# One transformer-like kernel: longer runs of context products in the MoE, and attention scores with both passes on all 128 rows

## The chip, the cores and the metric

The kernel runs on one core of a Trainium2 chip. Its time is the device time of one execution in microseconds (us), and the figure compared is the median of the runs. The engines are TensorE (PE in the rows, with PEld for its weight loads), VectorE (DVE), ScalarE (ACT), GpSimd (POOL) and SyncE (SP, which here only issues transfers).

## The reference, cut to what matters

A stream of 1024 latent tokens and a prefix of 256 context tokens, width 1024, goes through two layers. Layer 0 is a mixer of two linear-attention kinds, then an expert-choice mixture of experts (MoE) on the latent tokens and another on the context tokens. Layer 1 is windowed attention of the latent tokens, then the MoE on the latent tokens alone. The two pieces that the change touches are these:

```python
# attention, per block of 128 queries: window of 384 latent keys, 256 context keys, a sink
s_loc = where(valid, einsum('bqhgd,bshd->bhgqs', qb, kb), -inf)
s_ctx = einsum('bqhgd,bshd->bhgqs', qb, k_ctx)
p = softmax(concatenate([s_loc, s_ctx, sink_logit]))
out = einsum(p[..., :span], vb) + einsum(p[..., span:-1], v_ctx)
# MoE: 16 experts, each takes its top-C tokens: 128 latent ones, 32 context ones
hid = silu(xe @ w1) * (xe @ w3)
ye = (hid @ w2) * gate          # added back to the tokens' rows
```

There are 16 query heads of 64 dimensions, 4 key heads, and 8 blocks of queries; a key head serves 4 query heads.

## The kernel before, in words

**Products in two halves.** Large products are made in float32r: each operand is split into a high part (a rounded copy that ACT writes) and a low part (the operand less its high part, by DVE); `split_hl` (lines 1191 and 1192) does it for most. A product is then high x high + high x low + low x high. The context products of the MoE, the transposes and the product of probabilities and values are plain float32.

**MoE (class Moe).** For each of the 16 experts `up` goes over 8 k tiles of 128 rows. `tiles` (line 1519) loads the weights in raw tiles of 1 MB that hold two k tiles each, from SP's queue, into 8 buffers in layer 0. Each k tile of a weight is split into `uhi` and `ulo` (6 buffers each). Line 1580 makes the 12 products of the latent tokens per k tile, with 512 columns each. The context tokens are 32 rows only, so their product (line 1586) puts the array in four column groups of 32 and takes the raw, unsplit weights: 4 products per k tile, one to a group. They are made in runs: after every `CG` k tiles (line 1500) the products of these k tiles follow one another. `down` does the same with one weight (line 1637). A raw tile is free again when its context products are done. Down of expert e-1 follows up of expert e. After k tile 3 of an up, `between` transposes what the next steps need (the `ps_t` and `ps_x` tiles). The planner of the framework sets the order of the instructions there. Layer 1's MoE has no context tokens.

**Attention (class Attn).** `keys` loads the transposed keys and writes `k2`, the high part of a key head, twice: in rows 0 to 63 and in rows 64 to 127 (line 1758), and `kl`, the low part, once, in the half that the key head has (line 1759). `load_q` writes `q2` for a pair of key heads: the high part of the queries in one half of the rows (line 1883) and the low part in the other (line 1884). `probs` makes the scores of two heads in a step: a first pass of 128 rows, (high q over low q) x (k2 twice), and a second of 64 rows, high q x `kl`. A pass has two products, one for the window (up to 384 columns, line 1909) and one for the context (256 columns, line 1910). DVE adds the mask and takes the extreme (line 1917), ACT makes the exponential (line 1922) and normalises one head (line 1931), DVE or POOL the other (line 1930). `turn` transposes the probabilities by PE (line 1944) and copies them out by DVE and ACT (lines 1946, 1948). `mix` multiplies them with the values (line 1961), with the array in two column groups of 64. `out_tile` multiplies by the output weights (line 1352, 512 columns), and then normalises, transposes and routes (lines 1395 and 1403).

**The order of the attention.** PE's order is written out by hand in `run`: a loop of 64 + 12 steps. Step i makes the scores of step i, with the transposes of step i-2 put between, then one `mix_step`, one step of the output product, one step of the top-k search on DVE (lines 1428 to 1433). A mix covers two steps' probabilities; `mix_step` makes its first two chunks in one step of the loop and the rest in the next. The other engines' order is the planner's. The output weights are split in the first steps (`prep`, from step 3 on).

Of the kernel before, what the change touches and what calls it, by code (L numbers as in the profile page):

```python
# [10 lines left out]
F32R = mybir.dt.float32r  # L11
# [3 lines left out]
AF = mybir.ActivationFunctionType  # L15
# [5 lines left out]
NCTX = 256  # L21
NLAT = 1024
T = NCTX + NLAT
# [1165 lines left out]
def split_hl(K, hi, lo, src):  # L1189

    K.nc.scalar.activation(hi, src, AF.Copy)  # L1191
    K.nc.vector.tensor_sub(lo, src, hi)  # L1192
# [304 lines left out]


RAW1, UB1 = 13, 4
CG = 2  # L1500


class Moe:
# [221 lines left out]
class Attn:  # L1725
# [19 lines left out]
    def keys(self, part):  # L1745

        K, nc, p = self.K, self.K.nc, self.kp
        if part == 0:
            self.k2 = p.tile([128, 4, T], F32R, name="k2", bufs=1)
            self.kl = p.tile([128, 2, T], F32R, name="kl", bufs=1)  # L1750
        c = slice(640 * part, 640 * part + 640)
        for a in range(2):
            t = p.tile([128, 640], F32, name="kT", tag="kT", bufs=2)
            nc.sync.dma_start(t, dap(K.s_k[a], part * 5 * 16384, [[128, 128], [16384, 5], [1, 128]]))
            for par in range(2):
                r = slice(64 * par, 64 * par + 64)
                for half in range(2):
                    nc.scalar.activation(self.k2[64 * half:64 * half + 64, 2 * a + par, c], t[r], AF.Copy)
                nc.vector.tensor_sub(self.kl[r, a, c], t[r], self.k2[r, 2 * a + par, c])

    def norm(self, tt, mods, ps1):

# [111 lines left out]
    def load_q(self, n, pair):  # L1874

        K, nc, p = self.K, self.K.nc, self.kp
        t = p.tile([128, 4, 128], F32, name="qld", tag="qld", bufs=1)
        nc.sync.dma_start(t, dap(K.s_q, n * 128 * 1024 + 512 * pair, [[1024, 128], [128, 4], [1, 128]]))
        q2 = p.tile([128, 2, 4, 128], F32R, name="q2", tag="q2", bufs=2)
        yield  # L1880
        for g in range(2):
            r, o = slice(64 * g, 64 * g + 64), slice(64 * (1 - g), 64 * (1 - g) + 64)
            nc.scalar.activation(q2[r, g], t[r], AF.Copy)
            nc.vector.tensor_sub(q2[o, g], t[r], q2[r, g])
            yield
        yield q2

# [4 lines left out]
    def probs(self, n, g, jj, q2, ps):  # L1892

        K, nc, p = self.K, self.K.nc, self.p
        b0, b1, nl = self.window(n)
        k0, mo, nk = NCTX + 128 * b0, 128 if n == 0 else 0, nl + NCTX
        pair, gg = divmod(g, 2)
        pes = []
        st = p.tile([128, 5, 2], F32, name="ast", tag="ast", bufs=4)
        hr = slice(64 * gg, 64 * gg + 64)  # L1900
        h0 = 4 * g + 2 * jj
        for i_ in range(2):
            pe = p.tile([128, 640], F32, name="pe", tag="pe", bufs=PEB)
            pes.append(pe)

            sc = ps.tile([128, 1024], F32, name="ps_s", tag="sc")
            qa = q2[:, gg, 2 * jj + i_]
            for i, (l, r) in enumerate(((qa, self.k2[:, g]), (qa[hr], self.kl[hr, pair]))):
                nc.tensor.matmul(sc[:, 512 - nl:512], l, r[:, k0:k0 + nl], start=(i == 0), stop=(i == 1))  # L1909
                nc.tensor.matmul(sc[:, 512:768], l, r[:, 0:NCTX], start=(i == 0), stop=(i == 1))  # L1910
            low = self.sink[:, 1, h0 + i_:h0 + i_ + 1]
            if n < 7:
                parts = ((0, nk, mo),)
            else:
                parts = ((0, nl, 0), (nl, nk, 384))
            for a, b, m in parts:
                nc.vector.tensor_tensor_reduce(pe[:, a:b], sc[:, 512 - nl + a:512 - nl + b], self.mask[:, m:m + b - a],  # L1917
                                               1.0, low, OP.add, OP.min, st[:, 0, i_:i_ + 1])
                low = st[:, 0, i_:i_ + 1]
            yield  # L1920
        for i_ in range(2):
            nc.scalar.activation(pes[i_][:, :nk], pes[i_][:, :nk], AF.Exp, bias=st[:, 0, i_:i_ + 1], scale=-1.0,
                                 accum_out=st[:, 3, i_:i_ + 1])
            if i_:
                nc.vector.tensor_add(st[:, 2], self.sink[:, 0, h0:h0 + 2], st[:, 0])
                nc.scalar.activation(st[:, 2], st[:, 2], AF.Exp)
            yield
        nc.vector.tensor_add(st[:, 3], st[:, 3], st[:, 2])
        nc.vector.reciprocal(st[:, 4], st[:, 3])  # L1929
        (nc.vector if n < NV else nc.gpsimd).tensor_scalar(pes[0][:, :nk], pes[0][:, :nk], st[:, 4, 0:1], None, op0=OP.mult)  # L1930
        nc.scalar.activation(pes[1][:, :nk], pes[1][:, :nk], AF.Copy, scale=st[:, 4, 1:2])
        yield pes
# [19 lines left out]
    def mix(self, n, pair, jj, pTs):  # L1952

        K, nc = self.K, self.K.nc
        b0, b1, _ = self.window(n)
        chunks = [2 + b for b in range(b0, b1 + 1)] + [0, 1]
        po = self.av
        for c, ch in enumerate(chunks):
            for gg in range(2):
                g = 2 * pair + gg  # L1960
                nc.tensor.matmul(po[64 * gg:64 * gg + 64, 2 * jj:2 * jj + 2], self.v[:, ch, 64 * g:64 * g + 64],  # L1961
                                 pTs[gg][:, c], start=(c == 0), stop=(c == len(chunks) - 1), skip_group_check=True)
            if c in (1, len(chunks) - 1):
                yield

    def run(self, ps2, ps1, pso, out, fill, prep):

        p = self.p
        q2 = None
        live, mixes, outs, m, pg = [], [], [], {}, {}  # L1970
# [14 lines left out]
        def mix_step():  # L1985
            if not mixes:
                return
            mx, left, key, jj_ = mixes[0]
            if left == 2 and jj_ == 0:
                self.av = pso.tile([128, 4, 128], F32, name="ps_av", tag="av")  # L1990
            next(mx, None)
            mixes[0][1] -= 1
            if left == 1:
                mixes.pop(0)
                if jj_ == 1:
                    mh, ml = (p.tile([128, 4, 128], F32R, name=x, tag=x, bufs=3) for x in ("mh", "ml"))
                    split_hl(self.K, mh, ml, self.av)
                    m[key] = mh, ml
                    if key[1] == 1:
                        outs.append([out(key[0], [m.pop((key[0], x)) for x in range(2)]), 0])  # L2000

        ng = self.load_q(0, 0)
        for _ in range(3):
# [1 line left out]
        for i in range(64 + 12):  # L2005
            x, y = i - 1, i - 2
# [3 lines left out]
            if new:  # L2010
                n, pair, jj, gg = i // 8, i // 4 % 2, i // 2 % 2, i % 2
# [15 lines left out]
            if tg:  # L2027
                pT = next(tg)
# [5 lines left out]
            if tg:  # L2034
                if gg_ == 0:
                    first = pT
                else:
                    mixes.append([self.mix(ty, pair_, jj_, (first, pT)), 2, (ty, pair_), jj_])
            if i % 4 < 3:
                next(ng, None)  # L2040
            if i >= W0:
# [304 lines left out]
```

## Time and profile before

| what | value |
|---|---|
| median of 3 runs | 3565.34 us (3556.50 to 3571.91) |
| profiled execution | 3550.13 us, span 3548.4 us |
| PE busy | 3235.4 us, 91% |
| PE weight loads | 2395.0 us, 67% |
| DVE busy | 2419.9 us, 68% |
| ACT busy | 2073.3 us, 58% |
| POOL busy | 732.1 us, 21% |
| mean granted TensorE clock | 0.941 |
| matmuls of the context up / down (L1586 / L1637) | 126.0 us / 69.1 us busy |

Busy shares are means over stages. In the order of time they are: the head, the projection and the mixer of layer 0; the MoE of layer 0 from about 1474 to 2262 us, with the PE busy throughout; the projection of layer 1; the attention from about 2488 us; the top-k search; the MoE of layer 1 from about 2950 us; the last norm. A matmul's duration runs beyond the start of the next, since matmuls are pipelined, so what one costs is read from start to start. In float32 a matmul is shown as two records: the run of 8 context products stands as x16. A clock of 1.00 in a stretch is 2.4 GHz, and 0.50 is 1.2 GHz.

### The profile page before, as it was taken

To read this page: it belongs to the slowest core of one execution; us is meant where nothing else is said; L and a number is where in the kernel's file an instruction comes from. 1 tells how busy PE (TensorE), PEld (TensorE's weight loads), DVE (VectorE), ACT (ScalarE), POOL (GpSimd) and SP (SyncE) were. 2 spreads that over 40 slices of the span, in tenths; PEclk is the share of its full clock that TensorE was granted. 3 is DMA by queue.
4 is the path that set the end of the run, shared out by engine and by line. 5 is a ranking of instruction groups with operands and counts; after the bars stand their busy time and mean duration, and the time that the engine had idled before them with its cause. 6 is when DMAs were issued, how large, how long until landed. Compare 5 with 4: busy or idle time off the path is not lost. (4 is left out here: it accounts for less than half of the span.)

```text
span 3548.4 us, 60256 instructions
## 1 busy us (share of the span) xinstructions
PE 3235.4 (91%) x23392; PEld 2395.0 (67%) x23392; DVE 2419.9 (68%) x4034; ACT 2073.3 (58%) x3529; POOL 732.1 (21%) x716
## 2 busy tenths in 40 slices
PE   5999999995888888799999999799999977999997
PEld 3866667774777766566666666467667756888885
DVE  4277775577544468777777777534865687999998
ACT  4254554432444555576666666533677736888886
POOL 1133232232333343101110110011233310010101
PEclk9998999997999989899999999899699988999998
DMA  5265565666999764578888888562210148999995
GB/s 194 71 201 168 171 189 177 240 184 137 196 227 195 178 225 146 208 282 280 286 280 290 277 273 280 195 219 80 71 47 31 44 174 300 383 389 388 386 380 212
DMA packets 480161, 767.80 MB, mean 216 GB/s; under 512 B 231836, under 2 KB 318532, under 8 KB 472708
## 3 DMA queue, kind: packets, MB, share of 16 engines
q1 hardware_dynamic: 434640, 601.05, 51.4%
q0 software_dynamic: 41648, 151.55, 13.8%
q10 hardware_dynamic: 3587, 11.36, 1.0%
q8 instruction: 184, 3.01, 0.4%
q14 instruction: 102, 0.83, 0.1%
HBM read 631.48 MB, written 132.38 MB: 215 GB/s over the span
## 5 line engine op out<-in xcount | busy, mean ns | idle before, releaser
L1192 DVE TENSOR_TENSOR ulo<-raw,uhi 128x1024 fp32r<-128x1024 f32 x768 | 901.7, 1221 | 127.9 <-ACT uhi L1191 119.1
L1191 ACT ACTIVATE uhi<-raw 128x1024 fp32r<-128x1024 f32 x768 | 789.5, 1069 | 245.6 <-PE ps_y L1631 127.2
L1580 PE MATMUL ps_h<-uhi,xh 128*128 128x512 f32 x1024 | 334.0, 404 | 0.8 <-ACT uhi L1191 0.7
L1580 PE MATMUL ps_h<-ulo,xh 128*128 128x512 f32 x1024 | 320.8, 394 | 3.0 <-DVE ulo L1192 2.2
L1580 PE MATMUL ps_h<-uhi,xl 128*128 128x512 f32 x1024 | 319.5, 392 | 0.0
L1647 POOL DMA_INDIRECT s_x<-yo,idxl x31 | 49.2, 1587 | 977.3 <-DVE yo L1643 977.3
L1580 PEld LDWEIGHTS ps_h<-uhi,xh 128*128 128x128 f32 x1024 | 184.2, 189 | 73.1 <-ACT uhi L1191 20.8
L1580 PEld LDWEIGHTS ps_h<-ulo,xh 128*128 128x128 f32 x1024 | 190.6, 188 | 54.9 <-DVE ulo L1192 12.3
L1580 PEld LDWEIGHTS ps_h<-uhi,xl 128*128 128x128 f32 x1024 | 191.5, 188 | 41.6
L354 PE MATMUL ps_in<-hl,whi 128*128 128x512 f32 x512 | 171.8, 411 | 0.0
L354 PE MATMUL ps_in<-hh,wlo 128*128 128x512 f32 x512 | 169.4, 409 | 1.5 <-POOL wlo L338 1.5
L354 PE MATMUL ps_in<-hh,whi 128*128 128x512 f32 x512 | 169.3, 408 | 0.9 <-DVE convu L671 0.9
L1631 PE MATMUL ps_y<-uhi,th 128*128 128x512 f32 x512 | 167.2, 407 | 0.6 <-ACT tc L1617 0.5
L1631 PE MATMUL ps_y<-ulo,th 128*128 128x512 f32 x512 | 161.1, 395 | 0.1
L1631 PE MATMUL ps_y<-uhi,tl 128*128 128x512 f32 x512 | 158.6, 391 | 0.0
L1917 DVE CUSTOM_DVE_ANT_0 pe<-ps_s,amask,sink 128x640 f32<-128x640 f32 (+2 forms) x128 | 104.4, 816 | 68.2 <-PE ps_s L1910 66.5
L1930 POOL TENSOR_SCALAR pe<-pe,ast 128x640 f32<-128x640 f32 (+1 forms) x48 | 92.1, 1918 | 216.7 <-DVE ast L1929 195.2
L1553 ACT ACTIVATE xv<-ps_x,Gf 128x128 f32<-128x128 f32 x256 | 96.7, 471 | 66.6 <-PE ps_x L1549 66.6
L1586 PE MATMUL ps_hc<-raw,xc 128*32 128x512 f32 x1024 | 126.0, 599 | 0.0
L1631 PEld LDWEIGHTS ps_y<-uhi,th 128*128 128x128 f32 x512 | 91.2, 188 | 49.7 <-issue 20.1
L1352 PE MATMUL ps_out<-woh,mh 128*128 128x512 f32 x288 | 117.1, 452 | 1.1 <-ACT mh L1191 1.1
L821 DVE TENSOR_TENSOR invt<-invB,invX 128x112 f32<-128x112 f32 (+27 forms) x248 | 93.1, 375 | 29.1 <-DMA invB<-s_L 24.0
(509 smaller groups left out, 7294.1 us busy)
## 6 DMA issues: line engine op xcount, KB each, us to landing
raw<-in_moe_w_dram SPq DMA_DIRECT2D x384, 1024.0 KB
ada_w<-in_ada_w_dram SPq DMA_DIRECT2D x48, 1024.0 KB
wraw<-in_e_w_in_dram SPq DMA_DIRECT2D x32, 512.0 KB
s_rk<-arbk POOLq DMA_DIRECT2D x16, 1024.0 KB, 5.9
kq<-s_kq SPq DMA_DIRECT2D x20, 512.0 KB
s_x<-ox POOLq DMA_DIRECT2D x18, 512.0 KB
s_h<-ot POOLq DMA_DIRECT2D x18, 512.0 KB, 4.2
s_rkv<-rkv POOLq DMA_DIRECT2D x12, 640.0 KB, 3.8
```

The lines of the kernel that those rows point to most:

```text
L354: nc.tensor.matmul(ps, l[:, k, :], r[:, k, a:a + m], start=(k == 0 and n == 0), stop=(k == 7 and n == 2))
L821: nc.vector.tensor_mul(t, B[:N, k, k + 1:, None].to_broadcast([N, r, c]), X[:N, k, None, 0:c].to_broadcast([N, r, c]))
L1191: K.nc.scalar.activation(hi, src, AF.Copy)
L1192: K.nc.vector.tensor_sub(lo, src, hi)
L1352: nc.tensor.matmul(po[:, cp_], l, r[:, k, c_], start=(k == 0 and n == 0), stop=(k == 7 and n == 2))
L1553: nc.scalar.activation(v[:, q], pt[:, q], AF.Identity, bias=self.nrm[:, 1, k, 0:1], scale=self.nrm[:, 0, k, 0:1])
L1580: nc.tensor.matmul(pl[m][n], l[:, k], r[:, 512 * n:512 * n + 512], start=(k == 0 and i == 0), stop=(k == 7 and i == 2))
L1586: nc.tensor.matmul(pc[32 * g:32 * g + 32], xc[:, k_], rs[g // 2][:, 512 * (g % 2):512 * (g % 2) + 512], start=(k_ == 0), stop=(k_ == 7), s ...
L1631: nc.tensor.matmul(py[n], l[:, k], r[:, 512 * n:512 * n + 512], start=(k == 0 and i == 0), stop=(k == 7 and i == 2))
L1647: nc.gpsimd.indirect_dma_start(out=K.s_x[1], out_offset=bass.IndirectOffsetOnAxis(ap=idx[:, e:e + 1], axis=0), in_=yo, in_offset=None, com ...
L1917: nc.vector.tensor_tensor_reduce(pe[:, a:b], sc[:, 512 - nl + a:512 - nl + b], self.mask[:, m:m + b - a], 1.0, low, OP.add, OP.min, st[:, ...
L1930: (nc.vector if n < NV else nc.gpsimd).tensor_scalar(pes[0][:, :nk], pes[0][:, :nk], st[:, 4, 0:1], None, op0=OP.mult)
```

## The change

`CG` becomes 4, so that a run of context products covers four k tiles and there are two runs per up and two per down. `k2` of a key head holds the high part in the head's half of the rows and the low part in the other half; `kl` is gone. `q2` holds the high part of the queries in both halves, and in a second place the low part in both halves. Both score passes then have 128 rows: high q x (high k over low k), and low q x the same; the product low x low comes with it. `mix` makes all its chunks in one step, and `mix_step` loses its count of what is left.

```diff
-CG = 2
+CG = 4
...
             self.k2 = p.tile([128, 4, T], F32R, name="k2", bufs=1)
-            self.kl = p.tile([128, 2, T], F32R, name="kl", bufs=1)
...
             for par in range(2):
-                r = slice(64 * par, 64 * par + 64)
-                for half in range(2):
-                    nc.scalar.activation(self.k2[64 * half:64 * half + 64, 2 * a + par, c], t[r], AF.Copy)
-                nc.vector.tensor_sub(self.kl[r, a, c], t[r], self.k2[r, 2 * a + par, c])
+                r, o = slice(64 * par, 64 * par + 64), slice(64 * (1 - par), 64 * (1 - par) + 64)
+                nc.scalar.activation(self.k2[r, 2 * a + par, c], t[r], AF.Copy)
+                nc.vector.tensor_sub(self.k2[o, 2 * a + par, c], t[r], self.k2[r, 2 * a + par, c])
...
-        q2 = p.tile([128, 2, 4, 128], F32R, name="q2", tag="q2", bufs=2)
+        q2 = p.tile([128, 2, 2, 4, 128], F32R, name="q2", tag="q2", bufs=2)
         yield
         for g in range(2):
             r, o = slice(64 * g, 64 * g + 64), slice(64 * (1 - g), 64 * (1 - g) + 64)
-            nc.scalar.activation(q2[r, g], t[r], AF.Copy)
-            nc.vector.tensor_sub(q2[o, g], t[r], q2[r, g])
+            for x in (r, o):
+                nc.scalar.activation(q2[x, 0, g], t[r], AF.Copy)
+            for x in (r, o):
+                nc.vector.tensor_sub(q2[x, 1, g], t[r], q2[r, 0, g])
...
             sc = ps.tile([128, 1024], F32, name="ps_s", tag="sc")
-            qa = q2[:, gg, 2 * jj + i_]
-            for i, (l, r) in enumerate(((qa, self.k2[:, g]), (qa[hr], self.kl[hr, pair]))):
-                nc.tensor.matmul(sc[:, 512 - nl:512], l, r[:, k0:k0 + nl], start=(i == 0), stop=(i == 1))
-                nc.tensor.matmul(sc[:, 512:768], l, r[:, 0:NCTX], start=(i == 0), stop=(i == 1))
+            k2 = self.k2[:, g]
+            for i in range(2):
+                qa = q2[:, i, gg, 2 * jj + i_]
+                nc.tensor.matmul(sc[:, 512 - nl:512], qa, k2[:, k0:k0 + nl], start=(i == 0), stop=(i == 1))
+                nc.tensor.matmul(sc[:, 512:768], qa, k2[:, 0:NCTX], start=(i == 0), stop=(i == 1))
...
                                  pTs[gg][:, c], start=(c == 0), stop=(c == len(chunks) - 1), skip_group_check=True)
-            if c in (1, len(chunks) - 1):
-                yield
+        yield
...
-            mx, left, key, jj_ = mixes[0]
-            if left == 2 and jj_ == 0:
+            mx, key, jj_ = mixes.pop(0)
+            if jj_ == 0:
                 self.av = pso.tile([128, 4, 128], F32, name="ps_av", tag="av")
-            next(mx, None)
-            mixes[0][1] -= 1
-            if left == 1:
-                mixes.pop(0)
-                if jj_ == 1:
-                    mh, ml = (p.tile([128, 4, 128], F32R, name=x, tag=x, bufs=3) for x in ("mh", "ml"))
-                    split_hl(self.K, mh, ml, self.av)
...
+            next(mx)
+            if jj_ == 1:
+                mh, ml = (p.tile([128, 4, 128], F32R, name=x, tag=x, bufs=3) for x in ("mh", "ml"))
+                split_hl(self.K, mh, ml, self.av)
...
-                    mixes.append([self.mix(ty, pair_, jj_, (first, pT)), 2, (ty, pair_), jj_])
+                    mixes.append([self.mix(ty, pair_, jj_, (first, pT)), (ty, pair_), jj_])
```

## Rows read from the trace of the kernel before

**Rows 1.** Page, part 2: granted TensorE clock, in 40 slices of the span.

```profile
PEclk9998999997999989899999999899699988999998
```

**Rows 2.** Stretches: length; busy PE, PEld, DVE, ACT, POOL (count); clock; DMA share, GB/s.

```profile
1500.00:2250.00 750.00, 749.11 (x4549) 490.81 (x4549) 550.56 (x565) 509.25 (x714) 78.09 (x54) 1.00 0.80 275
2486.00:2554.00 68.00, 64.73 (x225) 42.23 (x225) 53.81 (x109) 41.56 (x88) 21.59 (x10) 0.50 0.29 72
2666.69:2715.44 48.75, 48.75 (x300) 34.31 (x299) 29.26 (x77) 35.77 (x85) 17.06 (x11) 1.00 0.13 44
2715.44:2765.74 50.30, 50.30 (x301) 35.52 (x299) 29.35 (x77) 35.77 (x85) 17.06 (x11) 0.97 0.12 43
2814.48:2860.54 46.06, 46.06 (x288) 33.14 (x287) 37.02 (x120) 30.60 (x76) 13.31 (x10) 1.00 0.11 35
```

**Rows 3.** Waits of SP's queue, 1500 to 2250 us: total, times, longest.

```profile
SPq L1519 <- PE ps_hc L1586: 456.4, 61, 9.8
```

**Rows 4.** PE timeline around one context run of an up: start, us, instruction.

```profile
1807.84 0.62 PE L1580 MATMUL ps_h<-ulo,xh 128*128 128x512 f32 x2
1808.30 0.61 PE L1580 MATMUL ps_h<-uhi,xl 128*128 128x512 f32 x2
1808.84 1.92 PE L1586 MATMUL ps_hc<-raw,xc 128*32 128x512 f32 x16
1810.70 0.74 PE L1580 MATMUL ps_h<-uhi,xh 128*128 128x512 f32 x2
1811.28 0.63 PE L1580 MATMUL ps_h<-ulo,xh 128*128 128x512 f32 x2
```

**Rows 5.** PE timeline, a context run of a down.

```profile
1839.48 1.07 PE L1637 MATMUL ps_yc<-raw,tc 128*32 128x256 f32 x16
1840.48 0.74 PE L1631 MATMUL ps_y<-uhi,th 128*128 128x512 f32 x2
```

**Rows 6.** Timeline, one head's scores behind transposes: first, second, what follows the fourth.

```profile
2675.12 0.42 PE L1909 MATMUL ps_s<-k,q 128*128 128x384 f32 x1
2675.38 0.28 PE L1910 MATMUL ps_s<-k,q 128*128 128x256 f32 x1
...
2676.07 0.88 PE L1944 MATMUL ps_pT<-ident,pe 128*128 128x128 f32 x6
```

**Rows 7.** Timeline with weight loads, 128-row scores behind the output product.

```profile
2679.83 0.34 PE L1909 MATMUL ps_s<-k,q 128*128 128x384 f32 x1
2679.83 0.19 PEld L1910 LDWEIGHTS ps_s<-k,q 128*128 128x128 f32 x1
...
2680.00 0.28 PE L1910 MATMUL ps_s<-k,q 128*128 128x256 f32 x1
```

**Rows 8.** PE timeline, last block of queries: scores, transposes, mix, output product.

```profile
2838.70 0.28 PE L1909 MATMUL ps_s<-k,q 128*128 128x256 f32 x1
2838.81 0.28 PE L1910 MATMUL ps_s<-k,q 128*128 128x256 f32 x1
...
2840.70 0.66 PE L1944 MATMUL ps_pT<-ident,pe 128*128 128x128 f32 x4
2841.28 1.08 PE L1961 MATMUL ps_av<-pT,v 128*64 128x256 f32 x8
2842.30 0.50 PE L1352 MATMUL ps_out<-woh,mh 128*128 128x512 f32 x1
2842.64 0.39 PE L1352 MATMUL ps_out<-wol,mh 128*128 128x512 f32 x1
```

**Rows 9.** PE timeline, the longer half of a mix.

```profile
2688.41 1.51 PE L1961 MATMUL ps_av<-pT,v 128*64 128x256 f32 x12
```

**Rows 10.** Groups of ACT, 2617.93 to 2666.69 us: the queries' high parts.

```profile
L1883 ACT ACTIVATE q<-qld 64x512 fp32r<-64x512 f32 x4 | 2.5, 624 | 0.0
```

**Rows 11.** PE timeline, first block of queries: a head's first score, the transposes behind it.

```profile
2497.64 0.56 PE L1909 MATMUL ps_s<-k,q 128*128 128x256 f32 x1
...
2499.07 1.11 PE L1944 MATMUL ps_pT<-ident,pe 128*128 128x128 f32 x4
```

More of the change, by code (lines that the diff above doesn't have):

```diff
@@ L1899, in probs @@
         st = p.tile([128, 5, 2], F32, name="ast", tag="ast", bufs=4)
-        hr = slice(64 * gg, 64 * gg + 64)
         h0 = 4 * g + 2 * jj
@@ L1987, in mix_step @@
                 return
-            mx, left, key, jj_ = mixes[0]
-            if left == 2 and jj_ == 0:
+            mx, key, jj_ = mixes.pop(0)
+            if jj_ == 0:
                 self.av = pso.tile([128, 4, 128], F32, name="ps_av", tag="av")
-            next(mx, None)
-            mixes[0][1] -= 1
-            if left == 1:
-                mixes.pop(0)
-                if jj_ == 1:
-                    mh, ml = (p.tile([128, 4, 128], F32R, name=x, tag=x, bufs=3) for x in ("mh", "ml"))
-                    split_hl(self.K, mh, ml, self.av)
-                    m[key] = mh, ml
-                    if key[1] == 1:
-                        outs.append([out(key[0], [m.pop((key[0], x)) for x in range(2)]), 0])
+            next(mx)
+            if jj_ == 1:
+                mh, ml = (p.tile([128, 4, 128], F32R, name=x, tag=x, bufs=3) for x in ("mh", "ml"))
+                split_hl(self.K, mh, ml, self.av)
+                m[key] = mh, ml
+                if key[1] == 1:
+                    outs.append([out(key[0], [m.pop((key[0], x)) for x in range(2)]), 0])
         ng = self.load_q(0, 0)
```

## The prediction

> **What bounds the kernel now.** I read the page's slices first, to see which stages run at the full clock, then busy time by stretch for the two stages that change, then the waits of SP's queue, and last the PE timeline, from start to start, at each place that the edits touch. The reader should see this. In layer 0's MoE the PE is busy for 749 of 750 us at a granted clock of 1.00, while DVE has 551 and ACT 509 us of work [rows 2]. SP's queue spends 456 of these 750 us waiting for a context run to free a raw tile [rows 3]. So the weights wait for the PE, not the other way round, and each us that the PE no longer spends is a us off the time. The attention is the same from the second block of queries on: a block of eight steps takes 48.75 us, all of it PE at 1.00, with 35.8 us of ACT and 29.3 us of DVE [rows 2]. Its first 68 us differ: the clock is at 0.50, which is 1.2 GHz, the PE is busy 64.7 us and DVE 53.8 us [rows 2]; it is the slice with a 6 in the clock's line [rows 1]. What comes after the attention (the last search, layer 1's MoE, the norm) is not changed and should only start earlier.
>
> **Context runs.** Two pairs of latent products follow each other at 0.46 us (1807.84 to 1808.30), so 0.23 us a product. The pair before a context run takes 0.54 us (1808.30 to 1808.84), so going into the run costs 0.08. The run itself takes 1.86 us (1808.84 to 1810.70). The first pair behind it takes 0.58 us, which is 0.12 more than a pair [rows 4]. A down's run has half the columns and takes 1.00 us [rows 5]. With t for the streaming of an up's run and f for what does not depend on columns, t + f = 1.86 and t/2 + f = 1.00, so t = 1.72 and f = 0.14. A run taken away by joining it to the next saves 0.08 + 0.14 + 0.12 = 0.34 us; the streaming stays. There are four runs per up and four per down now, two of each afterwards, so 16 x 4 = 64 go: 21.8 us. Could it be less? DVE and ACT split the weights in this stage, and without a run between k tiles 4 and 8 the PE comes to the last of them about 2 us sooner, just when ACT has the transposed operands to serve. With 30% of ACT and 27% of DVE idle [rows 2] I take off 1 us in all: 21. Bounds: 0, if each expert gains a wait of 1.4 us, and 22.
>
> The raw tiles are held longer: four of the eight buffers until the end of an up's run. Cover: the window moved 275 GB/s x 750 us = 206 MB in 0.80 x 750 = 600 us of DMA time [rows 2], so four tiles (4.2 MB) take 12.2 us. The PE works on four such tiles for 24 pairs x 0.46 + 2 x 1.72 + 0.34 = 14.8 us. The next four arrive within the group that runs meanwhile; margin 2.6 us. I cost this at nothing.
>
> **Scores.** Behind transposes a head with the full window takes 0.95 us (2675.12 to 2676.07), of which the first product takes 0.26 [rows 6]. Behind an output product, in the same shape and number format, that first product of 384 columns takes 0.17 us, 2679.83 to 2680.00 [rows 7], and a 128-row product of 256 columns that has another 128-row product behind it 0.11 us, 2838.70 to 2838.81 [rows 8]. In the changed kernel all four are of that kind: 0.26 + 0.11 + 0.17 + 0.11 = 0.65 us. So a head saves 0.30 us: the change of shape into the 64-row pass and out of it. The added product low x low costs nothing, since a pass streams the same columns whether 64 or 128 rows are filled. Of 128 heads, the 16 of the first block and 6 of the second run at 1.2 GHz; the other 106 save 31.8 us.
>
> **Mix.** Eight records take 1.02 us from start to the next start, and four more add 1.51 - 1.08 = 0.43 us, 0.108 each [rows 8, 9]. So 1.02 - 8 x 0.108 = 0.16 us is fixed. Going in costs 0.14 (four transposes at (0.88 - 0.66)/2 = 0.11 each are 0.44 us, and 0.58 us pass before the mix), coming out 0.34 - 0.23 = 0.11 [rows 4, 6, 8]. The step without a mix then pays what the first score pays behind transposes, 0.26 - 0.17 = 0.09. A joined mix saves 0.16 + 0.14 + 0.11 - 0.09 = 0.32 us; 27 of the 32 at full clock, 8.6 us. The output product of a block starts a step earlier; its operands of the first pair of key heads are split four steps before, so no wait is added.
>
> **What the other engines leave of it.** At full clock the PE gives back 31.8 + 8.6 = 40.4 us, of which a block of 48.75 us gets 16 x 0.30 + 4 x 0.32 = 6.1. `load_q` doubles: four more ACT copies a block at 0.62 us [rows 10] and as many subtractions on DVE. ACT then has 35.8 + 2.5 = 38.3 us in a block of 42.7, or 90%, in a chain (copy transposes, exponential, sum, normalise) that waits inside each step. It nearly becomes the bound, so I expect some of the PE's time to come back as waits before transposes whose buffer ACT has not emptied. Bounds: 18 us (half) and 40; I take 36, since 4.4 us of idle ACT a block remain. In the last block DVE is at 37.0 of 46.1 us because of the top-k search [rows 2]; that is within the same allowance, and the tail behind it, which ends on DVE's search, I cost at no change.
>
> **First 68 us.** At 1.2 GHz a head with 256 + 256 columns takes 1.43 us (2497.64 to 2499.07) [rows 11]. Four products at twice 0.107 are 0.85, and twice the 0.09 behind transposes makes 1.03: 0.40 saved, x 22 heads = 8.8 us, and five mixes give 2 or 3 more: 11. But DVE has only 68 - 53.8 = 14.2 us idle there [rows 2], and gets about six more subtractions, 4 us. So I take 8; bounds 0 and 12. If the clock rises sooner, DVE keeps it to the upper bound. `keys` has four ACT copies fewer before the first scores; at the 0.62 us of the nearest row [rows 10] at most 2.5 us, and I take 1.
>
> **Sum.** 21 + 36 + 8 + 1 = 66 us. Against the profiled execution's own 3550.1 us that is 3484. The median of the runs shown is 3565.3, 15 us above the profiled one; the same 66 us make it **3499 us**, which is the forecast.
>
> **The rivals.**
>
> A. *ACT becomes the attention's bound.* Speaking for it: 90% load and a chain with waits inside. Against: copies of queries and the transposes' scaling have slack of a step. Then only half of the 36 comes: 66 - 18 = 48, 3517 us.
>
> B. *Weight loads stay open between whole-array passes.* Each score product loads its own weights. If in the changed kernel such a load could not run under the product before it, because both use the same rows, three more openings per head of 0.09 us (what the first score pays) up to 0.19 us (a whole load, [rows 7]) would take back 0.27 to 0.57 of the 0.30. The scores' part of the 66 is about 34; it would be 3 at the one end, and at the other a loss of 0.27 x 128 = 35, so the time is between 3530 and 3568; middle 3545. Against: a load for the 256-column pass starts at 2679.83, together with the product before it, both with 128 rows, and the next product starts after 0.17 us [rows 7]. The Trainium skill, "TensorE: Matmul & The Clock Gate", Part 3, The mechanism, says that weight loads overlap running matmuls only when the row group differs. By that rule this rival would be the forecast; the trace does not agree with it, since the 0.19 us load there is hidden in the same row group.
>
> C. *The context runs bring nothing,* since tiles held longer make the PE wait 1.4 us per expert. For: half of the buffers are tied up. Against: the 2.6 us of margin above. 3520 us.
>
> D. *The clock rises at the attention's start* and ACT too has room: 14 us more than forecast, 3485 us.
>
> E. *Slower: the clock falls in the longer context runs.* Place: layer 0's MoE, where 3.6 us of products with 32 columns of output each now come before the transposes. A drop costs: one block of queries has a mean clock of 0.97 and takes 50.30 instead of 48.75 us, 1.55 us for one short drop [rows 2]. Time at 1.2 GHz costs half of itself, so with 66 us gained elsewhere and here the point from which it decides is 132 us at 1.2 GHz, 8 us per expert. A drop of 3.1 us behind each of two long runs is not enough; 12 us per expert would give 96 of loss, 3595 us. Against: 1.00 over the 750 us with 1.86 us runs [rows 2, 4].
>
> **How the numbers follow.** Forecast 0.66 (its own range 3486 to 3512), A 0.13, B 0.06, C 0.06, D 0.05, E 0.04. A difference under about 0.5%, 18 us, cannot be told from none here. The forecast, A, C, D and a third of B are faster than that: 0.92; the rest of B is the same: 0.04; E is slower: 0.04. The range from 3470 to 3540 holds the forecast, A, C and D and half of B, with room below for the full prices (22 + 40 + 12 + 2 = 76) and for the 15 us between the runs.
>
> **What would show it.** In the changed profile: context runs of 32 records, about 3.6 us in an up; the four score products of a head at about 0.65 us from start to start; a mix of 20 records at about 2.3 us in every second step; a block of eight steps at 42.7 to 44 us, with ACT near 90%; SP still waiting for context runs; layer 1's MoE unchanged in length. It would be wrong if a block stays above 46 us, if a weight load of a second pass stands open, if the PE shows idle time in layer 0's MoE, or if its clock leaves 1.00 there.

## The result, and the profile after

The changed kernel takes 3501.6 us (median; runs from 3492.5 to 3507.9), the kernel before, timed beside it, 3567.0 (3556.5 to 3571.9). The ratio is 0.9841, with a 95% interval from 0.9815 to 0.9867: 57 us faster, between 47 and 66; the two medians themselves lie 65 us apart. The forecast was 3499. The stages tell more than this agreement does: two terms of the sum were off, in opposite directions.

All stage lengths are read between PE starts in the profiles. In this table "MoE" runs from layer 0's first latent product to its last context product, "gap" from there to the first score, and "attention" from the first score to the end of the top-k search behind it. A block is one block of queries, eight steps of two heads.

| us | before | after | difference | forecast |
|---|---|---|---|---|
| up to layer 0's MoE (same code) | 1472.7 | 1479.2 | +6.5 | 0 |
| layer 0's MoE | 791.4 | 764.3 | -27.2 | -21 |
| gap | 223.9 | 225.2 | +1.3 | -1 |
| attention | 451.5 | 423.4 | -28.1 | -44 |
| of this: first two blocks | 94.3 | 85.6 | -8.7 | |
| of this: a full block at full clock | 48.76 | 46.22 | -2.54 | -6.1 |
| everything behind | 608.8 | 608.6 | -0.3 | 0 |

The first line is noise: over the profiles of all kernels tried here this unchanged stretch lies between 1467.9 and 1483.1 us. The MoE's length repeats to within 0.6 us (763.7 to 764.3 over seven profiles with the same context runs), so stages tell edits apart that whole times can't. Without the first line the stages sum to 54 us, inside the interval.

The clock's line of the page after; the slice that was at 6 in [rows 1], at the attention's start, is at 8:

```profile
PEclk9999999898989989799999999899899988999998
```

Three stretches of the changed kernel, columns as in [rows 2]: layer 0's MoE, the attention's first two blocks, and one full block.

```profile
1500.00:2230.00 730.00, 729.38 (x4583) 506.19 (x4580) 552.94 (x571) 513.66 (x720) 78.21 (x54) 1.00 0.79 286
2468.70:2554.27 85.57, 66.48 (x393) 53.35 (x394) 77.20 (x166) 63.94 (x137) 20.20 (x10) 0.82 0.26 69
2646.71:2692.93 46.22, 42.99 (x298) 35.15 (x297) 31.47 (x82) 37.50 (x89) 16.72 (x10) 1.00 0.14 47
```

The MoE is still all PE at 1.00. In the full block the PE has 42.99 us of work, close to the 42.7 forecast, but the block takes 46.22: 3.2 us of PE idle time that [rows 2] did not have. Waits of the PE in that block (total, times, longest):

```profile
PE ps_pT L1945 <- ACT pT L1949: 2.5, 4, 1.2
PE ps_pT L1945 <- ACT ohT L1398: 0.7, 1, 0.7
```

The PE stands before transposes (L1945), whose buffers ACT has not yet copied out (L1949), though ACT is busy for only 37.5 of 46.2 us. One such wait, PE and ACT of the changed kernel:

```profile
2682.55 0.34 PE L1910 MATMUL ps_s<-k,q 128*128 128x384 f32 x1
2682.73 0.28 PE L1911 MATMUL ps_s<-k,q 128*128 128x256 f32 x1
2682.84 0.34 PE L1910 MATMUL ps_s<-k,q 128*128 128x384 f32 x1
2683.02 0.28 PE L1911 MATMUL ps_s<-k,q 128*128 128x256 f32 x1
2683.14 0.60 PE L1945 MATMUL ps_pT<-ident,pe 128*128 128x128 f32 x4
...
2683.76 0.83 ACT L1932 ACTIVATE pe<-pe,ast 128x640 f32<-128x640 f32 x1 [1.00 <-DVE ast L1930]
...
2684.17 0.60 PE L1945 MATMUL ps_pT<-ident,pe 128*128 128x128 f32 x4
2684.49 0.57 ACT L1949 ACTIVATE pT<-ps_pT 128x512 f32<-128x512 f32 x1
2684.97 0.82 ACT L1923 ACTIVATE pe<-pe,ast 128x640 f32<-128x640 f32 x1
2685.12 0.44 PE L1945 MATMUL ps_pT<-ident,pe 128*128 128x128 f32 x2 [0.35 <-ACT pT L1949]
2685.49 2.38 PE L1962 MATMUL ps_av<-pT,v 128*64 128x256 f32 x20
...
2690.51 0.60 ACT L1949 ACTIVATE pT<-ps_pT 128x512 f32<-128x512 f32 x1 [1.66 <-PE ps_pT L1945]
```

The transposes of 2683.14 are ready early, but their copy stands on ACT behind the normalisation (L1932), which itself waits 1.00 us for DVE. The copy starts at 2684.49, and the third group of transposes, which needs that buffer, comes 0.35 late. In the next step, behind the mix, it is the other way round: ACT waits 1.66 us for the PE's transposes (2690.51). So ACT can hold the PE up while it is idle a fifth of the time: what counts is its order.

A head costs 0.59 us behind an output product (2682.55 to 2683.14) and 0.68 behind transposes (2683.49 to 2684.17), against 0.65 forecast, and no weight load stands open: the products start 0.18, 0.11, 0.18 and 0.12 us after one another. The joined mix is 20 records in 2.38 us.

Context runs of the changed kernel, answering to [rows 4, 5] (the down's run is 1837.79):

```profile
1828.01 0.61 PE L1580 MATMUL ps_h<-uhi,xl 128*128 128x512 f32 x2
1828.55 3.64 PE L1586 MATMUL ps_hc<-raw,xc 128*32 128x512 f32 x32
1832.12 0.73 PE L1631 MATMUL ps_y<-uhi,th 128*128 128x512 f32 x2
...
1837.24 0.61 PE L1631 MATMUL ps_y<-uhi,tl 128*128 128x512 f32 x2
1837.79 1.93 PE L1637 MATMUL ps_yc<-raw,tc 128*32 128x256 f32 x32
1839.65 0.73 PE L1631 MATMUL ps_y<-uhi,th 128*128 128x512 f32 x2
```

An up's run takes 3.57 us, against 2 x 1.86; a down's 1.86, against 2 x 1.00. SP's queue still waits for the context runs, as in [rows 3]:

```profile
SPq L1519 <- PE ps_hc L1586: 445.3, 62, 15.2
```

### The profile page after: what moved, and what is told of

Same layout as the page of the kernel before. It is cut to its first block, busy times and chain, and to the rows that moved or that the text cites. A ratio compares the mean times of both kernels' runs of the same rounds, so it can differ in the third digit from the quotient of the medians.

```text
span 3500.7 us, 60284 instructions
## 1 busy us (share of the span) xinstructions
PE 3147.4 (90%) x23392; PEld 2406.9 (69%) x23392; DVE 2429.3 (69%) x4066; ACT 2082.7 (59%) x3553; POOL 728.7 (21%) x716
## 5 line engine op out<-in xcount | busy, mean ns | idle before, releaser
L1931 POOL TENSOR_SCALAR pe<-pe,ast 128x640 f32<-128x640 f32 (+1 forms) x48 | 90.5, 1885 | 185.7 <-DVE ast L1930 88.1
L1945 PE MATMUL ps_pT<-ident,pe 128*128 128x128 f32 x608 | 96.5, 283 | 32.4 <-ACT pT L1949 13.7
L1918 DVE CUSTOM_DVE_ANT_0 pe<-ps_s,amask,sink 128x640 f32<-128x640 f32 (+2 forms) x128 | 103.4, 810 | 26.6 <-PE ps_s L1911 25.5
```

The lines of the kernel that those rows point to most:

```text
L1945: nc.tensor.transpose(pt[:, k, i_], pes[i_][:, 128 * (c + k):128 * (c + k) + 128], K.ident)
```

## The experiments

Theory at the start: the context runs' gain is larger than priced and stands by itself; in the attention the PE's saving is real, but ACT's chain takes part of it back. Rivals: the attention's price per head was wrong, or part of the MoE's gain came from another edit.

All runs in one table. Ratios are to the kernel before, timed on the same chip, and rows are compared by them: 3567.0 is its median beside the changed kernel, and beside the other runs it was 3555.2 (the three edits alone and the queries by two DMAs), 3558.7 (mix in halves, down's run of eight, gain), 3557.7 (last copy, the two combined ones) and 3553.2 (the last). "PE work" is the PE's busy time in a full block, and "ACT busy" that of ACT.

| kernel | median | ratio [95%] | MoE | block | PE work | ACT busy | attention |
|---|---|---|---|---|---|---|---|
| before | 3567.0 | 1 | 791.4 | 48.76 | 48.76 | 35.8 | 451.5 |
| after | 3501.6 | 0.9841 [0.9815, 0.9867] | 764.3 | 46.22 | 42.99 | 37.5 | 423.4 |
| context runs alone | 3522.2 | 0.9896 [0.9874, 0.9919] | 763.7 | 48.8 | | | 456.3 |
| scores alone | 3517.7 | 0.9891 [0.9861, 0.9920] | 791.7 | 45.23 | 44.27 | 37.7 | 419.4 |
| mix alone | 3545.7 | 0.9979 [0.9964, 0.9993] | 791.5 | 48.62 | 47.73 | 35.1 | 444.2 |
| after, queries by two DMAs | 3485.9 | 0.9800 [0.9780, 0.9820] | 763.9 | 45.33 | 42.78 | 34.6 | 412.1 |
| after, mix in halves | 3495.7 | 0.9822 [0.9801, 0.9842] | 763.9 | 45.24 | 44.29 | 37.7 | 420.9 |
| after, down's run of eight | 3492.8 | 0.9818 [0.9796, 0.9841] | 762.0 | 46.23 | | | 421.7 |
| after, gain on DVE | 3490.6 | 0.9818 [0.9790, 0.9847] | 763.7 | 46.27 | | | 420.9 |
| after, last copy on DVE | 3491.2 | 0.9810 [0.9785, 0.9835] | 763.9 | 44.48 | 42.65 | 35.7 | 417.9 |
| queries, halves, eight | 3481.0 | 0.9776 [0.9756, 0.9797] | 762.7 | 44.48 | 43.84 | 35.0 | 411.6 |
| the same, last copy on DVE | 3481.7 | 0.9787 [0.9762, 0.9813] | 760.1 | 44.58 | 43.93 | 33.5 | 409.7 |
| joined mix, lighter ACT | 3475.7 | 0.9785 [0.9756, 0.9813] | 762.0 | 43.69 | 42.44 | 32.9 | 405.1 |

Where the expectations speak of the first eight heads and the eight behind them, the lengths they give are those of the first two blocks, of 16 heads each.

**Context runs alone.**

```diff
-CG = 2
+CG = 4
```

> The kernel before with the context products in runs of four k tiles, and nothing else changed. Layer 0's MoE (first ps_h to last yc) took 791.5 us in the profile of before and 764.3 with the whole change. Theory (the PE bounds that stage, and each of the 64 switches taken away is worth 0.425 us, more than the 0.34 that I priced): the stage falls to 764 to 765 us, the attention stays as before (block 48.75 us), the kernel is 27 us faster. Rival (part of the 27 came from the other edits, and the price was right): the stage falls to about 770, the kernel 21 us faster. Rival (held tiles): no gain.

The stage is 763.7 us: the whole 27.7 come from this edit, 0.43 per run taken away. The rival at 0.34 falls, and so does the one of the held tiles. The period of an expert (from one expert's token transposes to the next) says it most exactly: 49.30 us before and 47.56 after, the same in twelve experts in a row; 1.74 for four runs is 0.435. By time it is 37 us (29 to 45), an interval that leaves the 27 out, and the other stages do not hold the difference: in this profile the attention is 4.8 us longer than before, since two of its full blocks ran at a clock of 0.93 and 0.97 (51.84 and 50.31 us) and the first two blocks took 96.1 us against 94.3. So a whole time can be some 10 us off what an edit does, and the attention's length some 5 us where the clock falls.

**Scores alone,** the new `keys`, `load_q` and `probs` in the kernel before:

```diff
-            qa = q2[:, gg, 2 * jj + i_]
-            for i, (l, r) in enumerate(((qa, self.k2[:, g]), (qa[hr], self.kl[hr, pair]))):
+            for i in range(2):
+                qa = q2[:, i, gg, 2 * jj + i_]
...
```

> The kernel before with the new keys, queries and score passes, and the mix and the context runs as before. By PE time alone a block at full clock falls by 16 heads x 0.30 = 4.8 us, to 43.95, and the whole is 31.8 us faster plus what the first 68 us give. Theory (the copies, transposes' buffers and in-order chain on ACT now end the block): about the same block as with the whole change, 46.2 to 46.8, so 12 to 18 us faster in all. Rival (PE time sets it): block 44 to 44.5, 30 to 38 us faster.

A full block and its PE waits:

```profile
2665.04:2710.27 45.23, 44.27 (x298) 34.91 (x297) 31.15 (x82) 37.68 (x89) 17.31 (x11) 1.00 0.14 48
```

```profile
PE ps_pT L1945 <- ACT pT L1949: 1.0, 2, 0.5
```

By time it is 39 us (28 to 49), near the rival, but the block missed both numbers: it is 45.23, a us *below* that of the whole change, with 44.27 us of PE work and only 1.0 of waits. ACT's load is the same as in the whole change (37.7 and 37.5), so ACT's load alone can't explain the 46.22. The scores' part of the attention is 32 us, more than the whole change's 28. What is left, the joined mix, must cost.

**Mix alone,** the new `mix` and `mix_step` in the kernel before:

```diff
-            if c in (1, len(chunks) - 1):
-                yield
+        yield
...
```

> The kernel before with the joined mix alone. The block there is all PE (48.75 us, PE busy throughout), so the price of 0.32 us a joined mix should come out in full: block 47.4 to 47.6, the kernel 8 to 12 us faster by itself. Rival (the joined mix needs its operands earlier and waits): block 48.75, no gain. With scores_alone it tells how the attention's gain divides: where the two together give more than the whole change does in the attention, the limit of ACT takes the difference.

```profile
2679.86:2728.48 48.62, 47.73 (x299) 34.56 (x297) 28.82 (x78) 35.12 (x85) 17.60 (x10) 1.00 0.12 44
```

```profile
PE ps_pT L1944 <- ACT pT L1948: 0.9, 2, 0.4
```

PE work falls by 1.03 us a block and 0.9 comes back as waits in a block that had none: 0.13 us gained where I expected 1.2 to 1.4. By time it is 7.5 us (2 to 13). In the attention as a whole it is 7.3 us, of which 1.55 is the one short clock drop of before's profile [rows 2], 2.6 lies in the first two blocks and 3.4 behind the last score.

**Mix in halves,** the other edits as changed:

```diff
-        yield
+            if c in (1, len(chunks) - 1):
+                yield
...
```

> The changed kernel with the mix in two halves again, as before the change; context runs of four and the new scores stay. By the two profiles already taken, a full block has 42.99 us of PE work and 3.2 us of PE waits with the joined mix (46.22), and 44.27 of work and 1.0 of waits with the scores changed alone (45.23). Theory (a joined mix makes the step without a mix too short for ACT, and what the PE saves comes back as waits before the transposes, with more): block 45.2 to 45.3, first score to the end of the top-k search about 419 us against 423.4, so 3 to 6 us faster than the changed kernel. Rival (what scores_alone showed came from the slower context runs or from another moment of the run): block 46.2 and no difference; or the price of 0.32 us a mix holds and this is 8 us slower.

```profile
2634.02:2679.26 45.24, 44.29 (x298) 34.95 (x297) 31.15 (x82) 37.68 (x89) 17.32 (x11) 1.00 0.13 48
```

The theory holds in the block: 45.24, as with the scores alone; joining the mix takes 1.30 us of PE work away and adds 2.3 of waits. Over the attention it is 2.5 us, and the expected 4 were not reached. The full blocks and the last one gain 5.5 us, but from the last score to the end of the search this kernel takes 70.1 us and the changed one 67.6, and its first two blocks took 86.1 us against 85.6. That end is the place where the joined mix does gain: it takes 66.8 to 68.3 us in all kernels with the joined mix and 70.1 to 70.5 in those with halves. In the whole times it can't be told from the changed kernel, since the intervals overlap.

**Queries loaded twice by DMA,** so that one copy and one subtraction fill both halves:

```diff
-        nc.sync.dma_start(t, dap(K.s_q, n * 128 * 1024 + 512 * pair, [[1024, 128], [128, 4], [1, 128]]))
+        for h in range(2):
+            nc.sync.dma_start(t[64 * h:64 * h + 64], dap(K.s_q, n * 128 * 1024 + 512 * pair,
+                                                        [[1024, 64], [65536, 2], [128, 4], [1, 128]]))
...
-            for x in (r, o):
-                nc.scalar.activation(q2[x, 0, g], t[r], AF.Copy)
-            for x in (r, o):
-                nc.vector.tensor_sub(q2[x, 1, g], t[r], q2[r, 0, g])
+            nc.scalar.activation(q2[:, 0, g], t[:, g], AF.Copy)
+            nc.vector.tensor_sub(q2[:, 1, g], t[:, g], q2[:, 0, g])
```

> The changed kernel, but the queries are loaded twice by DMA, into both halves of the partitions, so that one ACT copy and one subtraction per group of heads make the stacked operands: 4 ACT copies of 0.62 us and 4 subtractions fewer per block, as many as before the change. Theory (ACT's chain ends the block at 46.25 us while the PE has 43.0 us of work): block 44 to 45, 8 to 15 us faster than the changed kernel. Rival (the wait is the transposes' two buffers and the chain's latency, not ACT's load): block 46 to 46.3, no difference above 3 us.

```profile
2634.32:2679.65 45.33, 42.78 (x298) 35.19 (x297) 27.91 (x78) 34.59 (x85) 17.49 (x10) 1.00 0.19 59
```

The attention is 11.3 us shorter: 0.9 in each full block, 5.1 in the first two, where DVE also loses the doubled subtractions (80.5 us against 85.6). The block, 45.33, lies between the numbers of theory and rival: with the joined mix, 2.9 us less of ACT work a block are worth 0.9.

The same kernel a second time:

> A look at the kernel with the queries loaded twice by DMA a second time: block again 45.3 us, first score to the end of the top-k search 412 us, if those lengths repeat from one run to the next to within 1 us.

Block 45.35, attention 412.0, one run of 3488.7 us: lengths of this stage repeat to 0.1 us here.

**The last copy on DVE:**

```diff
-            if c == 2:
+            if c >= 2:
                 nc.vector.tensor_copy(pT[:, c:c + w], pt[:, :w])
```

> The changed kernel with the last copy of the transposed probabilities (128x256, 0.36 to 0.39 us, eight in a full block) on DVE instead of ACT. ACT's load in a block falls by about 3 us, as much as loading the queries twice took off it (2.9 us, block 46.22 to 45.33). Theory (ACT's load in its order is what holds the block): 45 to 45.4. Rival (it is the spacing of the steps, and the third pair of transposes waits for the first copy, which stays on ACT): 46 to 46.3. Other side: DVE, which sets the first 68 us, gets the copies there too, and the first two stretches of eight heads (38.1 and 47.5 us) get longer by 2 to 4 us.

```profile
2635.06:2679.54 44.48, 42.65 (x298) 35.19 (x297) 34.03 (x90) 35.72 (x81) 16.70 (x10) 1.00 0.14 49
```

The block falls by 1.74 us, more than either theory said. ACT's busy time falls by 1.8 us and not by 3, to 35.7, which is above that of the run with two DMAs (34.6). So it is not ACT's sum of work alone but which work: taking the last copies off its queue is worth twice as much as taking the queries' copies off. DVE's load does not explain it, since it rises here (31.5 to 34.0) and fell with the two DMAs (to 27.9). Nor are these the copies that the PE waits for. In the five full blocks of the changed kernel all 20 waits on L1949 stand before the third transposes of a step, for the first copy of that step, which stays on ACT here. The PE's waits on L1949 in the block go from 2.5 to 1.4 us:

```profile
PE ps_pT L1945 <- ACT pT L1949: 1.4, 2, 1.1
```

The other side did not come where it was expected: the first two blocks are as without the edit (85.9 and 85.6). It came in the last block, where DVE searches: that is 2.2 us longer (41.3 against 39.1 us from its first to its last score).

**A down's products in one run of eight tiles:**

```diff
-            if tc_ is not None and k % CG == CG - 1:
-                for k_, raw in raws[-CG:]:
+            if tc_ is not None and k == 7:
+                for k_, raw in raws:
```

> The changed kernel with all eight k tiles of a down in one context run: 16 more runs of layer 0's MoE go. Prediction's price, 0.34 us each: the stage falls from 764.3 by 5.4 us. What the whole change and cg_alone measured, 27.2 and 27.7 us for 64 runs, 0.43 each: by 6.8 us. Rival (all eight raw tiles held to the end of a down starve the weights): the stage gets longer, with PE idle before ps_h or ps_y.

762.0 us, 2 less instead of 5.4 or 6.8. In four experts the period is 47.17 to 47.20, which is 0.36 below 47.56 for the one run that goes; in others it is up to 48.18. ACT's wait for weights, in 1500 to 2230 us, was 6.3 us in the changed kernel; here it is

```profile
ACT uhi L1191 <- DMA raw<-in_moe_w_dram: 63.5, 41, 4.6
```

The PE meets this at the transposes of the next tokens (`ps_x`), not at `ps_h` or `ps_y` as the rival said:

```profile
PE ps_x L1549 <- ACT tc L1617: 1.0, 3, 0.5
```

The stage did not get longer, as the rival had it, but what the rival says of the held tiles, wrong for runs of four, begins here: the weights come late, ACT is late with its copies, and most of the price goes back. Four profiles with a down's run of eight have a stage of 760.1 to 762.7 us, so this length no longer repeats as it does with runs of four.

**The gain's multiplication on DVE:**

```diff
-            nc.gpsimd.tensor_mul(r, r, gain)
+            nc.vector.tensor_mul(r, r, gain)
```

> The changed kernel with the output weights' multiplication by the gain on DVE in place of POOL. In the first eight steps of the attention DVE's operations are up to 13 times as long while POOL multiplies (0.16 us becomes 2.20, 0.47 becomes 2.44). Theory (POOL's multiplication holds DVE up): the first eight heads, 38.1 us, and the eight behind them, 47.5, get shorter by 4 us or more together. Rival (the stretching is DVE's own queue, or the multiplication costs DVE as much as it frees): no change or longer, since DVE gets eight more operations of about 1.2 us.

The first block is 5.2 us shorter (32.9), the second 2.6 longer (50.1): together 83.0 against 85.6. The kernel with a down's run of eight, which has the same attention, took 83.8 there, so most of the 2.6 us is within what the start varies by. The stretching is gone (below); a gain in time is not shown.

**Together.** Queries by DMA, mix in halves, a down's run of eight:

> The changed kernel with three edits that each gained alone: queries loaded twice by DMA (first score to the end of the top-k search 412 us against 423), mix in halves (421, block 45.25), a down's context products in one run (stage 762 against 764.3). Theory (even steps and a lighter ACT add up): with 44.3 us of PE work a block the PE becomes the bound again, block 44.3 to 44.6, the attention to the end of the search 406 to 409, the whole 16 to 20 us faster than the changed kernel. Rival (both take away the same waits, 3.2 us a block, and the halves cost 1.28 of PE work): block 45.2 to 45.4, no better than the queries' edit alone.

```profile
2680.73:2725.21 44.48, 43.84 (x299) 34.96 (x298) 28.36 (x78) 35.04 (x85) 16.94 (x11) 1.00 0.21 60
```

The block is as the theory said: almost all PE, 0.6 us idle. The attention missed its 406 to 409: at 411.6 it is no better than with the queries' edit alone (412.1), as the rival said. The full blocks and the last one gain 5.2 us over that run, but the first two lose 1.3, and behind the last score, where halves cost time, 3.4 go. By ratio the whole is 23 us faster than the changed kernel.

> As the run before (queries twice by DMA, mix in halves, a down's products in one run), and the last copy of the transposed probabilities on DVE. If ACT still holds the block there, it falls by another 0.5 us or more; if the PE is the bound at 44.3 us of work, it stays, and the first 68 us get longer by what DVE takes there.

With the PE as the bound, less ACT work brings nothing: block 44.58. What was expected of the first 68 us didn't come: the first two blocks took 79.6 us against 81.8.

Last, the joined mix with both reliefs for ACT, the copy on DVE in the blocks 2 to 6 only (counted from 0), and with a down's run of eight. The copy's edit is now:

```diff
-            if c == 2:
+            if c == 2 or c == 4 and NV <= n < 7:
...
```

> The joined mix of the change, with two reliefs for ACT: queries loaded twice by DMA, and the last copy of the transposed probabilities on DVE in the blocks 2 to 6 only (DVE sets the first 68 us and the last block); a down's context products in one run as well. ACT has then some 33 us in a block, the PE 42.7 to 42.8. Theory (ACT's load in its order is all that kept the joined mix's 1.28 us a block from being seen): waits of 3.2 us shrink to 0.5 to 1, block 43.2 to 43.8, a us below the version with the mix in halves (44.47); first score to the end of the search 404 to 408 us; the whole 20 to 25 us faster than the changed kernel. Rival (the joined mix also makes steps of uneven length, and this part stays whatever ACT's load): block 44.4 or more, no better than in halves, 18 us faster than the changed kernel.

```profile
2667.23:2710.92 43.69, 42.44 (x299) 35.21 (x298) 30.48 (x86) 32.89 (x77) 16.69 (x10) 1.00 0.21 61
```

```profile
PE ps_pT L1944 <- ACT pT L1948: 1.1, 1, 1.1
```

The theory holds: 0.8 us a block below the mix in halves, which the rival excluded, with one wait of 1.1 us left. The attention is 405.1 us, 18.3 shorter than with the change as it was made. By time it is 76 us below the kernel before (interval 66 to 87). That is the lowest median tried but not the lowest ratio, and whole times don't part it from the two runs before it; their stages do (attention 405.1 against 411.6 and 409.7).

## Why the prediction was right, and where it was not

The total was right, and partly by luck. Two terms were off in opposite directions, 6 us too little in the MoE and 16 too much in the attention, and the stages give 54 us (27 + 28 - 1) for the 66 forecast. The rest of the agreement is chance of the medians, which lie 65 us apart within an interval of 47 to 66: before's profiled execution, on which the sum was made, lay 6 us below the lowest run timed beside the change.

*Context runs, 21 forecast, 27 measured.* The mechanism was right in all its parts (PE-bound, clock at 1.00, tiles in time), the price too low. I counted as the cost of a switch what the pair ahead of a run and the first one behind it show over a pair of 0.46 us [rows 4]. But the pairs settle slowly: fourteen from 1803.37 to 1809.72 in the changed kernel take 0.453 each, so twelve should take 5.44 us, and before they took 5.70 (1803.14 to 1808.84). In and out of a run thus cost 0.26, not 0.20, and with the fixed 0.14 that is 0.40, where the period of an expert says 0.435. For a down's runs the last switch showed 0.36 at its best.

*Scores, 0.30 a head.* With the scores alone a block's PE work falls from 48.76 to 44.27: 4.49 / 16 = 0.28. Right. Rival B falls with it: no load of a second pass stands open. The Trainium skill ("TensorE: Matmul & The Clock Gate", Part 3, The mechanism) would have weight loads overlap only where the row group differs; here whole-array products with loads of their own follow each other after 0.11 to 0.18 us, so the trace disagrees. The same section of the Trainium skill also lets a load into a background weight buffer go ahead of running products, and that the trace allows.

*Mix, 0.32 each.* As PE work this was exact: 44.29 to 42.99 in a block is 1.30 for four, 0.325 each; alone, in the kernel before, it was 1.03, or 0.26 each. As time it was worth 0.13 a block alone and cost 1.0 on top of the new scores. The step that failed is the sentence "so no wait is added", and with it "I take 36, since 4.4 us of idle ACT a block remain". I looked at the operands of the output product and not at the spacing. Two halves of a mix put 1.0 to 1.5 us of PE work into every step between one step's transposes and the next's; a joined one puts 2.4 into every second step and nothing into the others. Behind a step without one the PE comes early, and reaches the third transposes before ACT's queue has come through the first copy; behind a step with one it comes late, and ACT stands. ACT's share of 90% was the wrong measure: it came out at 81%, and the PE waited all the same.

*Attention as a whole.* At full clock it gave some 19 of the 36 (28.1 less the first two blocks' 8.7): 12.6 in five full blocks, 2.4 in the last one, 1.5 that are only the short clock drop in before's profile, and 2.8 behind the last score, which I had costed at no change. That is rival A's price, 18, for which I gave 0.13; and the prediction's own test, a block above 46 us, came true at 46.22. A's cause was half right: ACT's queue it is, as both reliefs of ACT show, but with the mix in halves the same load leaves 1.0 us of waits instead of 3.2.

*First 68 us, 8 forecast.* The first two blocks gave 8.7; 28 us of their 94.3 lie behind the 68. As foreseen the clock rose sooner (0.82 in place of a mean of 0.65 over the two) and DVE kept the rest, so rival D's clock came without its 14 us: the PE is now idle for 19 of 85.6 us, DVE busy for 77.

*Keys and gap, 1 forecast:* 1.3 longer, and from 219.8 to 225.2 over all runs, so nothing is shown. *Rival E:* the clock stayed at 1.00 through runs of 3.6 us. *Rival C:* not at four tiles, but begun at eight.

Open: why the last copies are worth twice the queries' copies, though the PE waits for neither. ACT's order is the reading that fits; it is argued and not shown, since neither another order of the same work on ACT nor a third buffer for the transposes was tried.

## What to carry to other kernels

Price work taken off the bounding engine from its busy time, but then ask in which steps the remaining work lies: here two engines that hand buffers back and forth lost time when one of them got uneven steps, with its partner only 81% busy. Where two edits aim at the same stage, time each alone: here one of them gave more than both. Price a switch of shapes from the whole stretch between two switches, or from the period of the loop, not from its neighbours.

## What the runs showed of the hardware

Some of DVE's operations stand still while POOL multiplies the output weights by the gain. In the attention's start, changed kernel:

```profile
2492.77 2.35 POOL L1275 TENSOR_TENSOR wstage<-wstage,ag 128x1024 f32<-128x1024 f32 x1 [15.01 <-DMA wstage<-in_o_w_out_dram]
2492.95 2.44 DVE L1931 TENSOR_SCALAR pe<-pe,ast 128x512 f32<-128x512 f32 x1
...
2496.35 2.63 POOL L1275 TENSOR_TENSOR wstage<-wstage,ag 128x1024 f32<-128x1024 f32 x1 [1.23 <-DMA wstage<-in_o_w_out_dram]
2496.80 2.20 DVE L1929 TENSOR_TENSOR ast<-ast 128x2 f32<-128x2 f32 x1
```

With the multiplication on DVE itself the same two are short:

```profile
2486.48 0.15 DVE L1929 TENSOR_TENSOR ast<-ast 128x2 f32<-128x2 f32 x1
...
2489.09 0.48 DVE L1931 TENSOR_SCALAR pe<-pe,ast 128x512 f32<-128x512 f32 x1
```

An addition of 128x2 elements takes 2.20 us in place of 0.15, and ends with POOL's multiplication (2499.00 and 2498.98). The Trainium skill ("SBUF — State Buffer", Who interferes with whom) says that DVE and GpSimd share a pair of ports, and that of two instructions which contend for it the one that issues second blocks until the first is done; these rows agree. DVE's busy time in such a stretch therefore holds time in which it only stood.

It is not all of DVE, and not every multiplication of POOL. Beside the same operation of POOL the score step (L1918), which reads PSUM, takes 0.73 us where it takes 0.74 or 0.75 elsewhere:

```profile
2473.09 4.67 POOL L1275 TENSOR_TENSOR wstage<-wstage,ag 128x1024 f32<-128x1024 f32 x2 [3.07 <-DMA wstage<-in_o_w_out_dram]
2475.58 0.73 DVE L1918 CUSTOM_DVE_ANT_0 pe<-ps_s,amask,sink 128x512 f32<-128x512 f32 x1
2476.23 1.80 DVE L1931 TENSOR_SCALAR pe<-pe,ast 128x512 f32<-128x512 f32 x1
```

Beside POOL's normalisation in the later blocks (L1931, 1.89 us in a full block) a small addition of DVE (L1926) takes its 0.15 us in all ten cases of the profile; only the five subtractions of queries (L1884) that start 0.1 us behind it take 1.24 in place of 0.69:

```profile
2649.09 1.89 POOL L1931 TENSOR_SCALAR pe<-pe,ast 128x640 f32<-128x640 f32 x1 [5.81 <-PE ps_pT L1945]
2650.21 0.15 DVE L1926 TENSOR_TENSOR ast<-sink,ast 128x2 f32<-128x2 f32 x1
```

Why the two multiplications of POOL differ is open.
